# Down projection of a feed-forward block: the readings of sums right behind their product, the tail's low parts behind the last reading

## The chip, the cores and the metric

The kernel runs on one core of one Trainium2 chip. The metric is the time of one execution in microseconds (us) on the device; lower is better. The core has five engines with a queue of instructions each: TensorE (PE, matrix products, with weight loads as PEld), VectorE (DVE), ScalarE (ACT), GpSimd (POOL) and SyncE (SP, here only an issuer of loads).

## The reference

Two layers, each a feed-forward block, a mixer of attention and retention, and a second feed-forward block, every one followed by a layer norm. 512 tokens, width 1024, inner width 2816.

```
def swiglu_ffn(x, w_gu, w_down):
    a, u = jnp.split(x @ w_gu, 2, axis=-1)
    return (jax.nn.silu(a) * u) @ w_down

for l in range(DEPTH):                       # DEPTH = 2
    x = layer_norm(ALPHA * x + 0.5 * swiglu_ffn(x, ffn1_w_gu[l], ffn1_w_down[l]), ln1_g[l], ln1_b[l])
    x = layer_norm(ALPHA * x + hybrid_mixer(x, ...), ln2_g[l], ln2_b[l])
    x = layer_norm(ALPHA * x + 0.5 * swiglu_ffn(x, ffn2_w_gu[l], ffn2_w_down[l]), ln3_g[l], ln3_b[l])
```

There are four feed-forward blocks in all, so four down projections (`@ w_down`), called D1 to D4 here. A mixer follows D1 and D3, the next layer's first feed-forward block follows D2, and nothing follows D4.

## The kernel before

**Split products.** Every float32 product is made of three matmuls: each operand is split into a high part (a cast on ACT, line 161) and a low part (a subtraction on DVE, line 162), and high x high, low x high and high x low are added in PSUM (lines 170 to 172). So each 128 x 1024 unit of weights costs one load into a raw tile (two raw buffers), one cast and one subtraction. The high part is named `uh`, the low part `ul`; `xh` and `xl` are the parts of the other operand.

**The weights' queue.** `Weights` holds the list of all units of the program. `get` hands out the next one, `done` gives buffers back, and both call `pump`, which issues casts and subtractions up to six units ahead (six unit buffers) and loads into raw tiles as they come free. A raw tile comes free when its last subtraction is done.

**The down projection.** The first 16 of 22 chunks of 128 rows are multiplied by a scheme of seven products on quarters of the matrices (numbered n = 0 to 6 in the loop of `ffn`), each of four groups of 12 matmuls with 512 columns. Some products add onto banks of PSUM that hold a sum already; before the bank is used for the next sum, `into` reads it into Y on DVE (line 726). These are the *readings*: two banks each after n = 1, 2, 3 and 5. The last, after n = 5, reads the two banks `low`. Behind product n = 5 PE runs chunk 16 (24 matmuls, the last six of which write `low`), then n = 6, chunk 17, and then the *tail*: chunks 18 to 21, of which each needs a unit of weights in a tail buffer (`tl`) and a split part of the hidden activations hT in a tile `hr`. Layer norm readings (line 459) follow bank by bank.

**The sums of weights.** The tiles R hold quarters of the matrix; POOL issues loads that add another quarter onto them (line 369) once the subtraction that used them is done.

**What sets the order.** Every engine works through its own queue in order. The order in the queues is set by the tile framework's scheduler when the program is built: from the first feed-forward block on (`self.pin = False`) it may move casts, subtractions and readings against each other where no data is in the way. A dependency without synchronisation (`add_manual_dep(..., NOSYNC)`) fixes the order of two instructions of one engine without a wait on a semaphore.

In the lists of instructions below, D1's tiles have these names: `ul_370` and `ul_380` are the low parts of chunks 16 and 17 (both from `raw_308`), `ul_383` and `ul_385` those of chunks 18 and 19 (from `raw_315`), `ul_388` and `ul_391` those of chunks 20 and 21 (from `raw_381`); `ul_372` to `ul_378` are the units of n = 6, `ul_362` to `ul_368` those of n = 5.

Of the kernel before, what the change touches and what calls it, by code (L numbers as in the profile page):

```python
# [10 lines left out]
ALU = mybir.AluOpType  # L11
# [18 lines left out]
GROUPS = 4  # L30
# [8 lines left out]
NOSYNC = mybir.DependencyInfo(mybir.DependencyClass.NoSync, mybir.DependencyReason.DATA)  # L39
# [55 lines left out]
class Trunk:  # L95
# [61 lines left out]
        lo = pool.tile([P, 1024], F32R, tag=tag + "l", name=self.nm("ul"), **kw)  # L157
        return hi, lo

    def split(self, hi, lo, src):  # L160
        a = self.nc.scalar.copy(hi, src)  # L161
        b = self.nc.vector.tensor_sub(lo, src, hi.bitcast(F32))  # L162
        if self.pin:
            self.tc.keep_in_program_order(a)
            self.tc.keep_in_program_order(b)
# [91 lines left out]
    def rows_item(self, w, r0, key, pools, heads=False):  # L257

        def load():
            v = self.raw().rearrange("p (c n) -> p c n", c=2)  # L260
            if heads:
                for kv in range(2):
                    q0 = kv * 256 + r0 // 2
                    self.nc.sync.dma_start(v[kv * HD : (kv + 1) * HD],
                                           w[q0 : q0 + P, :].rearrange("(c p) n -> p c n", p=HD))
            else:
                self.nc.sync.dma_start(v, w[r0 : r0 + 256, :].rearrange("(c p) n -> p c n", p=P))
            return v

        def cut(c):  # L270
            def go(v, hi, lo):
                self.split(hi, lo, v[:, c, :])
                return hi, lo
            return go

        return [(key, load, pools[c], cut(c)) for c in range(2)]
# [205 lines left out]
    def ffn(self, g_, b, out=None):  # L482
        nc, tc, W = self.nc, self.tc, self.W
        with ExitStack() as ctx:
# [4 lines left out]
            hT = hpool.tile([P, NF, SEQ], F32, name=self.nm("hT"))  # L489
# [94 lines left out]
            for fp in range(NFP):  # L584
                if fp == 0:
# [4 lines left out]
                    more = []  # L590
# [46 lines left out]
            def part(m, i, j):  # L637

                f = (j * GROUPS + 2 * m) * 2
                return hT[:, f : f + 4, i * 256 : (i + 1) * 256]  # L640

            def operand(src):

                k = slots[0] = (slots[0] + 2) % KC
                f = src.shape[1]
                hh, hl = (v[:, k : k + 2, :].rearrange("p k t -> p (k t)").rearrange("p (f t) -> p f t", f=f)
                          for v in (self.xh, self.xl))
                self.split(hh, hl, src)
                h = f // 2
                return [(hh[:, q * h : q * h + h], hl[:, q * h : q * h + h]) for q in range(2)]  # L650
# [3 lines left out]
            def fifth(m):  # L654

                a11, a21, a22 = part(m, 0, 0), part(m, 1, 0), part(m, 1, 1)
                nc.vector.tensor_sub(s1, a21, a22)
                nc.vector.tensor_sub(a21, a11, a21)
                nc.vector.tensor_sub(a11, s1, a11)
                return operand(s1)  # L660

            def third(m):

                nc.vector.tensor_add(part(m, 0, 1), part(m, 0, 1), part(m, 0, 0))
                return operand(part(m, 0, 1))

            def operands():
                ms = range(GROUPS // 2)
                for m in ms[1:]:
                    yield from operand(part(m, 0, 1))  # L670
                for m in ms:
                    yield from operand(part(m, 0, 0))
                for m in ms:
                    yield from fifth(m)
                for m in ms:
                    yield from operand(part(m, 0, 0))
                for m in ms:
                    yield from third(m)
                for m in ms:
                    yield from operand(part(m, 1, 0))  # L680
                chunks = operand(hT[:, FIRST : FIRST + 2, :])
                yield chunks[0]
                for m in ms:
                    yield from operand(part(m, 1, 1))
                yield chunks[1]
                for f in range(NF - TAIL, NF, 2):
                    room = pool.tile([P, 2, 2, 512], F32R, tag="hr", name=self.nm("hr"), bufs=2)
                    self.split(room[:, 0], room[:, 1], hT[:, f : f + 2, :])
                    for q in range(2):
                        yield room[:, 0, q : q + 1], room[:, 1, q : q + 1]  # L690

            def seventh(banks, u, h, new):

                for i, b_ in enumerate(banks):
                    ts = slice(i * P, (i + 1) * P)
                    for f in range(2):
                        self.mm3(b_, (h[0][:, f, ts], h[1][:, f, ts]), (u[0][:, f, :], u[1][:, f, :]),
                                 new and f == 0, False, skip_group_check=True)
                self.step()

            def down(f, u, h, t, q):
# [3 lines left out]
                         skip_group_check=True)  # L705

            split = operands()
            ahead = [(hv[0][:, g], hv[1][:, g]) for g in range(2)] + [next(split)]

            def chunk(f):  # L710
                u, h = W.get(), ahead.pop(0)
                ahead.append(next(split))
                for i, (t, q) in enumerate(((0, 0), (0, 1), (1, 0), (1, 1), (2, 1), (3, 1), (2, 0), (3, 0))):
                    down(f, u, h, t, q)
                    if i % 4 == 3:
                        self.step()
                W.done()
# [4 lines left out]
            def into(banks, t0, q, scale, sign=ALU.add):  # L722

                for i, b_ in enumerate(banks):
                    y = self.Y[:, t0 + i, q * 512 : (q + 1) * 512]
                    nc.vector.scalar_tensor_tensor(out=y, in0=y, scalar=scale, in1=b_, op0=ALU.mult, op1=sign)  # L726

            for n, (banks, new, more) in enumerate((
                    (left, True, None), (low, True, (0, 0, ALPHA)), (high, True, (0, 1, ALPHA)),
                    (low, False, (0, 1, 1.0, ALU.subtract)), (right, True, None),  # L730
                    (low, False, (2, 1, ALPHA, ALU.subtract)), (low, False, None))):
                if n == 6:
                    chunk(FIRST)
                for g in range(GROUPS):
                    u, h = W.get(), ahead.pop(0)
                    ahead.append(next(split))
                    seventh(banks, u, h, new and g == 0)
                    W.done(2 if n == 0 and g == 1 else 1)
                if more:
                    into(banks, *more)  # L740
            for f in range(FIRST + 1, NF - TAIL):
                if f == FIRST + 1:
                    gb = self.load_ln(self.spool, g_, b, "S", 2)
# [397 lines left out]
```

## Time and profile before

| | |
|---|---|
| time, median of 3 runs | 1792.26 us (1791.44 to 1794.13) |
| the profiled execution | 1792.29 us, its span 1790.4 us |
| PE busy | 1767.3 us of the span (99%) |
| DVE busy | 1386.6 us (77%) |
| ACT busy | 906.4 us (51%) |
| POOL busy | 162.7 us (9%) |
| granted TensorE clock, mean | 0.998 |
| bytes read from HBM | 206.09 MB |

The span is from the first to the last instruction of the profiled execution; the rest of its time, 1.9 us, lies around it. Rows of a timeline have the start in us from the span's start, the length in us, engine, line, operation, output <- input, shape, count, and in brackets the engine's idle time before and what ended it. `SPq` and `POOLq` mark instructions that issue loads. The last fields of a row of stretches are the granted clock, the share of the DMA engines and GB/s. Spans overlap a little: a matmul is listed as 0.39 us long while the next one starts 0.23 us after it, and a subtraction as 1.22 us with the next one 1.14 us behind.

### The profile page before, as it was taken

How to read it: one execution, taken by the hardware profiler on the slowest of the kernel's cores; microseconds unless marked ns; L12 is line 12 of the kernel's file. 1: busy time of each engine (PE TensorE's matmuls, PEld its weight loads, DVE VectorE, ACT ScalarE, POOL GpSimd, SP SyncE). 2: the span in 40 equal slices, each digit the busy share in tenths (PEclk: the TensorE clock that was granted, in tenths of full speed). 3: DMA queues.
4: the chain of work that ended last, by engine and by line, in shares of the span. 5: the costliest groups of instructions: out<-in, count | busy, mean ns of one | idle time of the engine just before them, and what ended most of it. 6: DMA issues, size and time to landing. Idle time of an engine off the chain costs nothing.

```text
span 1790.4 us, 29087 instructions
## 1 busy us (share of the span) xinstructions
PE 1767.3 (99%) x11978; PEld 1611.0 (90%) x11978; DVE 1386.6 (77%) x1926; ACT 906.4 (51%) x1423; POOL 162.7 (9%) x136
## 2 busy tenths in 40 slices
PE   9999999999999999999999999999999999999998
PEld 9999987887789999998799999889877899999876
DVE  7888888656767888879688887877667687888884
ACT  5455555278722455556235555553785234555550
POOL 0000031111111000012000000301011100000211
PEclk9999999999999999999999999999999999999999
DMA  6234397223222232389313324961323122244961
GB/s 188 95 102 135 120 228 172 88 83 90 52 95 71 86 127 95 95 241 181 118 58 98 106 95 165 224 175 42 99 79 94 48 95 95 95 129 131 217 136 48
DMA packets 158326, 210.07 MB, mean 117 GB/s; under 512 B 4848, under 2 KB 116208, under 8 KB 158192
## 3 DMA queue, kind: packets, MB, share of 16 engines
q1 hardware_dynamic: 140784, 174.64, 30.3%
q0 software_dynamic: 17408, 33.56, 10.5%
q8 instruction: 94, 1.54, 0.4%
q14 instruction: 40, 0.33, 0.1%
HBM read 206.09 MB, written 2.10 MB: 116 GB/s over the span
## 4 chain that ended last, share of the span: by engine, by line
PE 73%; DVE 10%; issue 7%; DMA 4%; ACT 4%; POOL 1%; SPq 0%; POOLq 0%; DVEq 0%; ACTq 0%
PE ps L170 23%; PE ps L171 23%; PE ps L172 23%; DVE ul L162 4%; DMA R<-in_ffn_w_down_dram 2%; DVE xl L162 2%; ACT uh L161 1%; PE ps L435 1%; DMA raw<-in_ffn_w_down_dram 1%; ACT sw L910 1%; DMA raw<-in_ffn_w_gu_dram 1%; ACT b L952 1%; ACT b L946 1%; DVE Y L726 1%; POOL R L369 0%
## 5 line engine op out<-in xcount | busy, mean ns | idle before, releaser
L170 PE MATMUL ps<-xh,uh 128*128 128x256 f32 (+1 forms) x1616 | 482.1, 298 | 0.0
L172 PE MATMUL ps<-xh,ul 128*128 128x256 f32 (+1 forms) x1616 | 479.1, 297 | 0.9 <-DVE ul L162 0.9
L171 PE MATMUL ps<-xl,uh 128*128 128x256 f32 (+1 forms) x1616 | 478.7, 296 | 0.2 <-DVE xl L162 0.2
L161 ACT CAST uh<-raw 128x1024 fp32r<-128x1024 f32 (+1 forms) x285 | 249.2, 894 | 247.9 <-PE ps L171 136.8
L162 DVE TENSOR_TENSOR ul<-raw,uh 128x1024 fp32r<-128x1024 f32 (+1 forms) x285 | 287.6, 1024 | 87.8 <-ACT uh L161 87.5
L170 PE MATMUL ps<-Th,uh 128*128 128x256 f32 x1152 | 319.1, 277 | 0.0
L171 PE MATMUL ps<-Tl,uh 128*128 128x256 f32 x1152 | 318.7, 277 | 0.0
L172 PE MATMUL ps<-Th,ul 128*128 128x256 f32 x1152 | 318.3, 276 | 0.0
L170 PEld LDWEIGHTS ps<-xh,uh 128*128 128x128 f32 x1616 | 307.9, 191 | 10.5 <-issue 1.6
L172 PEld LDWEIGHTS ps<-xh,ul 128*128 128x128 f32 x1616 | 307.8, 191 | 9.8 <-DVE ul L162 1.3
L171 PEld LDWEIGHTS ps<-xl,uh 128*128 128x128 f32 x1616 | 308.0, 191 | 8.4 <-DVE xl L162 0.8
L170 PE MATMUL ps<-uh,xh 128*128 128x512 f32 x672 | 265.1, 394 | 8.2 <-DVE Y L726 8.2
L171 PE MATMUL ps<-ul,xh 128*128 128x512 f32 x672 | 262.2, 390 | 0.0
L172 PE MATMUL ps<-uh,xl 128*128 128x512 f32 x672 | 261.9, 390 | 0.0
L161 ACT CAST uh<-S 128x1024 fp32r<-128x1024 f32 x144 | 151.2, 1050 | 149.0 <-PE ps L171 145.1
L162 DVE TENSOR_TENSOR ul<-S,uh 128x1024 fp32r<-128x1024 f32 x144 | 175.9, 1221 | 60.1 <-ACT uh L161 59.5
L171 PEld LDWEIGHTS ps<-Tl,uh 128*128 128x128 f32 x1152 | 216.7, 188 | 0.0
L170 PEld LDWEIGHTS ps<-Th,uh 128*128 128x128 f32 x1152 | 216.7, 188 | 0.0
L172 PEld LDWEIGHTS ps<-Th,ul 128*128 128x128 f32 x1152 | 216.3, 188 | 0.0
L369 POOL DMA_DIRECT2D R<-in_ffn_w_down_dram x64 | 77.7, 1216 | 994.7 <-DVE ul L162 959.0
L170 PEld LDWEIGHTS ps<-uh,xh 128*128 128x128 f32 x672 | 126.5, 188 | 38.2 <-DVE Y L726 9.9
L172 PEld LDWEIGHTS ps<-uh,xl 128*128 128x128 f32 x672 | 126.4, 188 | 26.6
(143 smaller groups left out, 2391.5 us busy)
## 6 DMA issues: line engine op xcount, KB each, us to landing
raw<-in_ffn_w_gu_dram SPq DMA_DIRECT2D x86, 1024.0 KB, 5.4
R<-in_ffn_w_down_dram POOLq DMA_DIRECT2D x64, 512.0 KB, 7.4
raw<-in_ffn_w_down_dram SPq DMA_DIRECT2D x20, 1024.0 KB, 5.1
raw<-in_w_in_dram SPq DMA_DIRECT2D x18, 1024.0 KB, 5.2
R<-in_ffn_w_down_dram SPq DMA_DIRECT2D x16, 1024.0 KB, 6.4
raw<-in_w_in_dram SPq DMA_DIRECT2D x8, 512.0 KB, 4.6
raw<-in_w_out_dram SPq DMA_DIRECT2D x8, 512.0 KB, 6.2
raw<-in_w_out_dram SPq DMA_DIRECT2D x4, 1024.0 KB, 4.9
```

The source lines that it names most:

```text
L161: a = self.nc.scalar.copy(hi, src)
L162: b = self.nc.vector.tensor_sub(lo, src, hi.bitcast(F32))
L170: mm(out, ah, bh, start=start, stop=False, **kw)
L171: mm(out, ah, bl, start=False, stop=False, **kw)
L172: mm(out, al, bh, start=False, stop=stop, **kw)
L369: self.nc.gpsimd.dma_start(src, rows(i, j, g * 256, 256), accum_op=ALU.add))
L435: nc.tensor.transpose(b[:, c * P : (c + 1) * P], src[:, c * P : (c + 1) * P], self.ident)
L726: nc.vector.scalar_tensor_tensor(out=y, in0=y, scalar=scale, in1=b_, op0=ALU.mult, op1=sign)
L910: nc.scalar.copy(sw[q * 32 : q * 32 + 32, :n], src[o * 32 : o * 32 + 32, :n])
L946: nc.scalar.activation(s[kv][:, cc, :nk], s[kv][:, cc, :nk], AF.Exp, bias=m[:, cc : cc + 1], scale=SCALE, accum_out=den[:, cc : cc + 1])
L952: nc.scalar.activation(s[kv][:, cc, :nk], s[kv][:, cc, :nk], AF.Copy, scale=den[:, cc : cc + 1])
```

## The change

Two edits. `into` is called before `W.done` of a product's last group, so before the units that `W.done` pumps are issued. And the subtractions for the low parts of the tail (the units of chunks 18 to 21, and the two `hr` tiles) get a dependency that places them behind the latest reading recorded at the time they are written, with no semaphore.

```
-    def split(self, hi, lo, src):
+    def split(self, hi, lo, src, behind=None):
         a = self.nc.scalar.copy(hi, src)
         b = self.nc.vector.tensor_sub(lo, src, hi.bitcast(F32))
+        if behind is not None:
+            self.tc.add_manual_dep(b.ins, behind.ins.name, NOSYNC, reason="the reading goes first")
...
-                self.split(hi, lo, v[:, c, :])
+                self.split(hi, lo, v[:, c, :], self.reading if pools[c] == self.tail_units else None)
...
-                    self.split(room[:, 0], room[:, 1], hT[:, f : f + 2, :])
+                    self.split(room[:, 0], room[:, 1], hT[:, f : f + 2, :], self.reading)
...
-                    nc.vector.scalar_tensor_tensor(out=y, in0=y, scalar=scale, in1=b_, op0=ALU.mult, op1=sign)
+                    self.reading = nc.vector.scalar_tensor_tensor(out=y, in0=y, scalar=scale, in1=b_, op0=ALU.mult,
+                                                                  op1=sign)
...
                     seventh(banks, u, h, new and g == 0)
+                    if more and g == GROUPS - 1:
+                        into(banks, *more)
                     W.done(2 if n == 0 and g == 1 else 1)
-                if more:
-                    into(banks, *more)
```

The order of PE's and POOL's instructions is the same in both programs. On DVE, ACT and SP it differs in the four down projections alone, and on DVE at the start of the third feed-forward block too.

DVE in D1, up to the last reading (the two SCALAR_TENSOR_TENSOR), before:

```order
L162 TENSOR_TENSOR xl_78<-hT_14_145,xh_77 128x1024
L162 TENSOR_TENSOR hr_389_3302<-hT_14_145,hr_389_3302 128x1024
L162 TENSOR_TENSOR ul_370_3145<-raw_308_2671,uh_369_3144 128x1024
L162 TENSOR_TENSOR hr_396_3343<-hT_14_145,hr_396_3343 128x1024
L162 TENSOR_TENSOR xl_78<-hT_14_145,xh_77 128x1024
L162 TENSOR_TENSOR ul_372_3163<-R_311_2700,uh_371_3162 128x1024
L162 TENSOR_TENSOR ul_374_3179<-R_311_2700,uh_373_3178 128x1024
L162 TENSOR_TENSOR xl_78<-hT_14_145,xh_77 128x1024
L162 TENSOR_TENSOR ul_376_3197<-R_312_2702,uh_375_3196 128x1024
L162 TENSOR_TENSOR ul_378_3215<-R_312_2702,uh_377_3214 128x1024
L726 SCALAR_TENSOR_TENSOR Y_79<-Y_79,ps_324_2782 128x512
L726 SCALAR_TENSOR_TENSOR Y_79<-Y_79,ps_326_2784 128x512
```

The same place on DVE after the change, and what stands behind the reading now:

```order
L162 TENSOR_TENSOR ul_374_3179<-R_311_2700,uh_373_3178 128x1024
L162 TENSOR_TENSOR xl_78<-hT_14_145,xh_77 128x1024
L162 TENSOR_TENSOR ul_376_3197<-R_312_2702,uh_375_3196 128x1024
L162 TENSOR_TENSOR ul_378_3215<-R_312_2702,uh_377_3214 128x1024
L728 SCALAR_TENSOR_TENSOR Y_79<-Y_79,ps_324_2782 128x512
L728 SCALAR_TENSOR_TENSOR Y_79<-Y_79,ps_326_2784 128x512
L162 TENSOR_TENSOR ul_383_3265<-raw_315_2737,uh_382_3264 128x1024
L162 TENSOR_TENSOR ul_380_3233<-raw_308_2671,uh_379_3232 128x1024
L162 TENSOR_TENSOR ul_385_3281<-raw_315_2737,uh_384_3280 128x1024
L162 TENSOR_TENSOR hr_389_3302<-hT_14_145,hr_389_3302 128x1024
L162 TENSOR_TENSOR hr_396_3343<-hT_14_145,hr_396_3343 128x1024
```

Six subtractions moved from ahead of the last reading to behind it: the two hr from among the ten before it, and the four of chunks 18 to 21 from further up (two ahead of the reading after n = 3, two between the two readings). The two readings after n = 1, which had a subtraction between them, now stand side by side. On ACT the two casts of chunks 20 and 21 moved as well, from ahead of the last two casts of n = 5 to behind the cast of chunk 17.

SP at the end of D2, before (`raw_1115` holds chunks 20 and 21; the `gu` loads are the next feed-forward block's):

```order
L267 DMA raw_1115_8667<-in_ffn2_w_down_dram 128x2x1024
L191 DMA raw_1120_8717<-in_ffn1_w_gu_dram 128x8x256
L448 DMA ln_1129_8772<-in_ln3_g_dram 128x1024
L449 DMA ln_1129_8772<-in_ln3_b_dram 128x1024
L191 DMA raw_1126_8754<-in_ffn1_w_gu_dram 128x8x256
L191 DMA raw_1135_8810<-in_ffn1_w_gu_dram 128x8x256
```

And after:

```order
L450 DMA ln_1129_8772<-in_ln3_g_dram 128x1024
L451 DMA ln_1129_8772<-in_ln3_b_dram 128x1024
L269 DMA raw_1115_8669<-in_ffn2_w_down_dram 128x2x1024
L193 DMA raw_1120_8717<-in_ffn1_w_gu_dram 128x8x256
L193 DMA raw_1126_8754<-in_ffn1_w_gu_dram 128x8x256
L193 DMA raw_1135_8810<-in_ffn1_w_gu_dram 128x8x256
```

The two loads of the layer norm's parameters went ahead of the tail's load. `raw_1115` now takes the buffer of chunks 16 and 17 and waits for chunk 17's subtraction, `raw_1120` that of chunks 18 and 19, `raw_1126` waits for chunk 21's subtraction, and `raw_1135` for the last one from `raw_1120`.

DVE at the end of D2, after the change, from the subtractions of chunks 20 and 21 to the layer norm's first two readings (line 461 there):

```order
L162 TENSOR_TENSOR ul_1122_8732<-raw_1115_8669,uh_1121_8731 128x1024
L162 TENSOR_TENSOR ul_1125_8751<-raw_1115_8669,uh_1124_8750 128x1024
L162 TENSOR_TENSOR ul_1128_8769<-raw_1120_8717,uh_1127_8768 128x1024
L162 TENSOR_TENSOR ul_1132_8803<-raw_1126_8754,uh_1131_8802 128x1024
L162 TENSOR_TENSOR ul_1134_8807<-raw_1120_8717,uh_1133_8806 128x1024
L162 TENSOR_TENSOR ul_1137_8813<-raw_1126_8754,uh_1136_8812 128x1024
L461 SCALAR_TENSOR_TENSOR Y_79<-Y_79,ps_1054_8211 128x512
L463 BN_STATS st_1141_8846<-Y_79 128x6
L162 TENSOR_TENSOR ul_1140_8819<-raw_1135_8810,uh_1139_8818 128x1024
L162 TENSOR_TENSOR ul_1168_9014<-raw_1135_8810,uh_1167_9013 128x1024
L461 SCALAR_TENSOR_TENSOR Y_79<-Y_79,ps_1055_8212 128x512
```

Before, both subtractions from `raw_1135` stood ahead of the norm's first reading; now they stand between its first and its second. Further on, the first norm reading of the fourth token block, which stood ahead of the second pair of `xl` that the third feed-forward block starts with, moved behind it.

## The prediction

> **What bounds the kernel now.** I read the page first, then the waits of PE, then PE's timeline where it waits, and from there back through DVE, ACT, POOL and DMA.
>
> ```profile
> span 1790.4 us, 29087 instructions
> PE 1767.3 (99%) x11978; PEld 1611.0 (90%) x11978; DVE 1386.6 (77%) x1926; ACT 906.4 (51%) x1423; POOL 162.7 (9%) x136
> ...
> raw<-in_ffn_w_gu_dram SPq DMA_DIRECT2D x86, 1024.0 KB, 5.4
> ```
>
> PE is the bound: it is idle for 23.1 us in all. The order of PE's own instructions is not touched, so time can come only from its waits. The largest of these (engine, what it waited for, total us, times, longest) is:
>
> ```profile
> engine line waited for: us in total, times, longest us
> PE ps L170 <- DVE Y L726: 8.2, 4, 3.5
> ```
>
> Line 726 is the reading of a sum; four waits, one in each down projection (D1 to D4), all at the last reading, whose two banks chunk 16 writes next. PE's rows (start, length, [idle before]):
>
> ```profile
> 302.62 0.39 PE L172 MATMUL ps<-uh,xl 128*128 128x512 f32 x1
> 305.02 0.50 PE L170 MATMUL ps<-uh,xh 128*128 128x512 f32 x1 [2.01 <-DVE Y L726]
> 305.36 0.39 PE L171 MATMUL ps<-ul,xh 128*128 128x512 f32 x1
> ...
> 852.68 0.39 PE L172 MATMUL ps<-uh,xl 128*128 128x512 f32 x1
> 855.11 0.50 PE L170 MATMUL ps<-uh,xh 128*128 128x512 f32 x1 [2.04 <-DVE Y L726]
> ...
> 1188.55 0.39 PE L172 MATMUL ps<-uh,xl 128*128 128x512 f32 x1
> 1189.63 0.50 PE L170 MATMUL ps<-uh,xh 128*128 128x512 f32 x1 [0.69 <-DVE Y L726]
> ...
> 1737.32 0.39 PE L172 MATMUL ps<-uh,xl 128*128 128x512 f32 x1
> 1741.21 0.80 PE L170 MATMUL ps<-uh,xh 128*128 128x512 f32 x1 [3.50 <-DVE Y L726]
> 1741.80 0.63 PE L171 MATMUL ps<-ul,xh 128*128 128x512 f32 x1
> ...
> 1744.35 0.40 PE L171 MATMUL ps<-ul,xh 128*128 128x512 f32 x1
> ...
> 1741.20:1744.00 2.80, 2.79 (x7) 2.22 (x8) 1.69 (x2) 0.00 (x0) 0.00 (x0) 0.50 0.09 35
> ```
>
> Undisturbed, one matmul of 512 columns follows another in 0.227 us, so D1's next was due at 302.85: 2.17 lost, and 0.11 more on the first matmul (305.02 to 305.36), 2.28. D2 alike: 2.20 + 0.11 = 2.31. D3: 0.85 + 0.11 = 0.96. D4: 3.66, and then seven matmuls take 3.14 instead of 1.59, since the granted clock is 0.50 in that stretch (the last line, sixth figure before the DMA's): 1.55 more, 5.21. **Sum 10.76.**
>
> **Why the reading is late.** DVE, POOL and ACT before the last reading of D1, and one row of each in D4:
>
> ```profile
> 286.45 2.36 DVE L162 TENSOR_TENSOR ul<-raw,uh 128x1024 fp32r<-128x1024 f32 x2 [0.89 <-ACT uh L161]
> 291.79 1.23 DVE L162 TENSOR_TENSOR ul<-R,uh 128x1024 fp32r<-128x1024 f32 x1 [1.84 <-ACT uh L161]
> 294.07 1.22 DVE L162 TENSOR_TENSOR hr<-hT,hr 128x1024 fp32r<-128x1024 f32 x1
> 295.20 1.22 DVE L162 TENSOR_TENSOR ul<-raw,uh 128x1024 fp32r<-128x1024 f32 x1
> 302.02 2.35 DVE L162 TENSOR_TENSOR ul<-R,uh 128x1024 fp32r<-128x1024 f32 x2
> 304.29 1.27 DVE L726 SCALAR_TENSOR_TENSOR Y<-Y,ps 128x512 f32<-128x512 f32 x2
> ...
> 281.37 1.22 POOL L369 DMA_DIRECT2D R<-in_ffn_w_down_dram  x1 [2.20 <-DVE ul L162]
> 290.71 1.05 ACT L161 CAST uh<-R 128x1024 fp32r<-128x1024 f32 x1 [1.45 <-DMA R<-in_ffn_w_down_dram]
> ...
> 1716.37 1.21 POOL L369 DMA_DIRECT2D R<-in_ffn_w_down_dram  x1 [2.19 <-DVE ul L162]
> 1723.10 2.00 ACT L161 CAST uh<-raw 128x1024 fp32r<-128x1024 f32 x2 [5.21 <-DMA raw<-in_ffn_w_down_dram]
> 1740.48 1.27 DVE L726 SCALAR_TENSOR_TENSOR Y<-Y,ps 128x512 f32<-128x512 f32 x2
> ```
>
> From 291.79 on DVE runs without a gap; the reading is a matter of what is queued ahead. PE would allow it at 299.0: the sixth product's last matmul lies 18 matmuls (4.08 us) before the one at 302.62.
>
> **The change, part by part.**
>
> *Two hr subtractions leave the queue ahead of the last reading.* Each takes 1.13 (294.07 to 295.20). If nothing else moved, the reading of D1 would start at 302.02 and its first bank be free at 302.70 (0.68 each), 0.15 before PE's 302.85. D2 (late by 2.20) and D3 (0.85) are covered by the same 2.27. D4 would keep 3.66 - 2.27 = 1.39 and, with a gap as short as those of D1 and D2, no half clock. So this alone is worth 10.76 - 1.39 = 9.4: the low end.
>
> *Four raw subtractions leave too, two of them with their casts.* On ACT the casts of the last tail pair waited for their load (5.21 in D4) with the casts of the sums R behind them; now they stand behind all of these. The last accumulating load (POOL, 281.37) waited for a subtraction behind two of the raw ones and can start up to 2.27 earlier, and no tail load runs beside it. It took 9.3 us to land (281.37 to 290.71). From its landing to the reading lie a cast and its subtraction (2.4), seven more subtractions (8.0) and about 1.1 us in which one of them waits for ACT: 11.5 us. D4's was issued at 1716.37, so the reading could start at 1716.4 - 2.3 + 9.3 + 11.5 = 1734.9, 2 us before it is needed; D1's at 299.9, 2 us as well. I take the whole 10.76, since D4 lost its time to that 5.21, not to the two hr. High end: the same.
>
> *The first readings stand together,* so one subtraction between them comes 0.6 later. Its product starts 5 us afterwards (three products of 48 matmuls, 10.9 us each, before 298.9 is 266.3): 0. The layer norm's two small loads now stand ahead of the tail load on SP; what they wait for, a sum's last split, comes before what the tail load waits for: 0.
>
> *What is late next: the tail's last pair and the next stage's weights.* Six subtractions follow the reading, and the load of the last tail pair now waits for the second of them. In D1: readings over at 300.3, load out at 302.7, landed (5.4 by the page) at 308.1, split by 310.5. PE wants it after chunk 16, four groups and chunk 17 (298.9 + 5.4 + 10.9 + 5.4 = 320.7): 10 us of cover. But the next stage's loads queue on its buffers. Rows of D2's end, in which the next stage is another feed-forward, and of D1's, with the mixer behind:
>
> ```profile
> 856.81 9.08 SPq L191 DMA_DIRECT2D raw<-in_ffn_w_gu_dram  x2
> 862.05 2.00 ACT L161 CAST uh<-raw 128x1024 fp32r<-128x1024 f32 x2 [4.19 <-DMA raw<-in_ffn_w_gu_dram]
> 871.20 1.05 ACT L161 CAST uh<-raw 128x1024 fp32r<-128x1024 f32 x1 [5.17 <-DMA raw<-in_ffn_w_gu_dram]
> 878.59 0.69 DVE L459 SCALAR_TENSOR_TENSOR Y<-Y,ps 128x512 f32<-128x512 f32 x1 [1.30 <-PE ps L172]
> 895.28 1.28 DVE L162 TENSOR_TENSOR xl<-ps,xh 128x512 fp32r<-128x512 f32 x2
> 896.52 0.28 PE L170 MATMUL ps<-xh,uh 128*128 128x256 f32 x1
> 896.64 0.28 PE L171 MATMUL ps<-xl,uh 128*128 128x256 f32 x1
> ...
> 306.73 6.02 SPq L229 DMA_DIRECT2D raw<-in_w_in_dram  x4
> 312.39 1.05 ACT L161 CAST uh<-raw 128x1024 fp32r<-128x1024 f32 x1 [1.92 <-DMA raw<-in_w_in_dram]
> 324.10 1.23 DVE L162 TENSOR_TENSOR ul<-raw,uh 128x1024 fp32r<-128x1024 f32 x1 [4.18 <-ACT uh L161]
> 325.75 0.69 DVE L459 SCALAR_TENSOR_TENSOR Y<-Y,ps 128x512 f32<-128x512 f32 x1 [0.42 <-PE ps L172]
> 328.47 0.69 DVE L459 SCALAR_TENSOR_TENSOR Y<-Y,ps 128x512 f32<-128x512 f32 x1 [1.30 <-PE ps L172]
> ```
>
> D1: the mixer's second load follows the tail pair's split (310.5, or 311.5 with ACT between), lands 5.6 later (306.73 to 312.39) at 317.1; the third follows the first's split (314.2), lands by about 319.5; the last subtraction ahead of the norm ends at 323.1. The norm's first reading may start at 325.75 - 2.28 = 323.5, its second has 1.30 of idle ahead. No lag: 0, with over 1 us to spare. D3 is the same program; D4 has no next stage.
>
> D2: three loads in a chain. Tail pair out at 852.6, landed 858.0, split 861.4; second out 861.5, landed (5.2, 856.81 to 862.05) 866.7, first two splits by 870.3; third out, landed (5.6, the second issue of the first row, 865.5, to 871.20) at 876.0, split 877.0 to 879.3. Those last two subtractions stand ahead of the norm's second reading, which PE would allow at 878.59 - 2.31 = 876.3: a lag of 3.0, or 4.2 if the tail pair lands 1.2 later beside its neighbour. From there DVE is dense to the xl at 895.28, whose second half ends at 896.56 and is wanted 12 matmuls of 0.12 after 896.52: 1.4 of slack, and the new order has one reading less ahead of it, 0.7 more. So PE waits 3.0 - 2.1 = 0.9 to 2.1 at the start of the third feed-forward: I take 1.3, nearer to the loads as measured one at a time. Bounds: 0 and 4.
>
> **Sum.** 1792.29 (the profiled execution: span 1790.4 and 1.9 around it; the runs' median 1792.26 is the same) - 10.76 + 1.3 = **1782.8 us**.
>
> **A rule weighed.** The row says 0.50 of the clock after 3.66 us without work and full clock after 2.2. The Trainium skill, "TensorE: Matmul & The Clock Gate", Part 1, has the clock halve after an idle window of about 3.4 us that runs freely, so that it depends on phase. The row agrees with the length; on the phase one execution shows nothing. By the row the change is worth 10.76; by the rule a run of before can miss the half clock, and the first rival below is what the time would then be.
>
> **The rivals.**
> - *No half clock in the timed runs.* It hangs on something that differs between executions: 1.55 less to win, 1792.26 - 9.2 + 1.3 = 1784.4. For it: the three runs spread over 2.7 us. Against: median and profiled time agree to 0.03.
> - *Nothing is given back.* D2's loads land faster than one after another at 5.4: lag under 2.1. 1792.29 - 10.76 = 1781.5. For it: DMA is nearly free there. Against: the chain of three has no slack in my sum.
> - *More is given back.* Each landing of the chain takes 0.75 longer: lag 5.9, wait 3.7 at D2's end, D1 and D3 still covered. 1785.2; with a half clock behind it, 1787.
> - *No change.* The accumulating loads land 2 us later than before, not earlier, and hold the cast that DVE needs (as 1.45 at 290.71): the readings stay late, 1792. Against: the load that ran beside them is gone.
> - *Slower.* The next stage's weights become the wait everywhere: each load takes the 9.3 us of the accumulating one. D1 and D3 then lag 3.7 (wait 3.2 each), D2's three loads lag 14.6 (wait 12.5, and 1.5 of half clock): 1792.29 - 10.76 + 20.4 = 1801.9. It turns slower once these waits pass 10.8 together, landings of about 7.7. For it: the chain is real. Against: 5.2 and 5.6 were measured in just that place.
>
> **How the numbers follow.** Likeliest 0.46 (1782.8, own range 1781.8 to 1784); no half clock 0.06; nothing given back 0.25; more given back 0.14; no change 0.05; slower 0.04. The range 1781 to 1787 takes the first four and the low end of the gain (9.4). A difference under 0.2% (3.6 us) can't be told from none: faster 0.91, same 0.05, slower 0.04.
>
> **What the profile after would show.** PE's waits on the reading gone, or one of about 1 us in D4; no stretch at half clock in D4; the last readings starting within 1 us of PE's release; the first xl of the third feed-forward ending after PE wants it, by 1 to 2 us, and no such wait before the mixers. I would be wrong if the readings still wait behind casts of R, or if a wait on ul or xl of over 4 us opens at a stage's start.

## The result and the profile after

| | before | after |
|---|---|---|
| median of six runs each, same chip (us) | 1794.38 | 1782.22 |
| lowest and highest (us) | 1791.44, 1799.89 | 1781.79, 1782.69 |
| profiled execution (us) | 1792.29 | 1781.79 |
| its span, PE busy (us) | 1790.4, 1767.3 | 1780.0, 1764.5 |

The ratio is 0.9932, 95% interval 0.992 to 0.9944: 0.7% faster, by 12.2 us between the medians and 10.5 between the profiled executions. The prediction was 1782.8. The runs of the kernel after lie within 0.9 us of each other, those of before within 8.5; that is a second difference, which a second profile of before, below, explains. Two later executions stand far outside, one of before (1926.2 us) and one with 128 unused bytes (7130.8), and no ratio below counts them.

The page and PE's list of waits, after (what PE waited for, total us, times, longest):

```profile
span 1780.0 us, 29097 instructions
PE 1764.5 (99%) x11978; PEld 1609.9 (90%) x11978; DVE 1387.0 (78%) x1926; ACT 906.7 (51%) x1423; POOL 162.8 (9%) x136
...
PE ps L985 <- DVE yal L162: 2.1, 2, 1.1
PE ps L429 <- POOL ident masks.py:199: 1.4, 1, 1.4
...
PE ps L173 <- DVE xl L162: 0.4, 2, 0.3
PE ps L174 <- DVE ul L162: 0.4, 2, 0.2
```

The row of 8.2 us on the readings is gone; the mixer's own wait (2.1) leads the list. PE at the place of the former gap in D1 and D4 (start, length), then its granted clock in D4 (the figure of 1.00 behind the busy time):

```profile
302.37 0.39 PE L174 MATMUL ps<-uh,xl 128*128 128x512 f32 x1
302.60 0.39 PE L172 MATMUL ps<-uh,xh 128*128 128x512 f32 x1
...
1732.16 0.39 PE L174 MATMUL ps<-uh,xl 128*128 128x512 f32 x1
1732.39 0.39 PE L172 MATMUL ps<-uh,xh 128*128 128x512 f32 x1
...
1732.00:1736.00 4.00, 4.00 (x19) 1.00 0.61 191
```

The matmul that had waited follows its forerunner in 0.23, in D2 and D3 too, and nothing runs at half clock. Why, from DVE in D1, and the last reading of D4:

```profile
297.08 1.23 DVE L162 TENSOR_TENSOR ul<-R,uh 128x1024 fp32r<-128x1024 f32 x1 [0.23 <-ACT uh L161]
298.23 1.28 DVE L728 SCALAR_TENSOR_TENSOR Y<-Y,ps 128x512 f32<-128x512 f32 x2
299.42 3.49 DVE L162 TENSOR_TENSOR ul<-raw,uh 128x1024 fp32r<-128x1024 f32 x3
302.83 2.36 DVE L162 TENSOR_TENSOR hr<-hT,hr 128x1024 fp32r<-128x1024 f32 x2
...
1728.88 1.28 DVE L728 SCALAR_TENSOR_TENSOR Y<-Y,ps 128x512 f32<-128x512 f32 x2
...
1714.65 1.05 ACT L161 CAST uh<-R 128x1024 fp32r<-128x1024 f32 x1 [1.50 <-DMA R<-in_ffn_w_down_dram]
1737.33 2.00 ACT L161 CAST uh<-raw 128x1024 fp32r<-128x1024 f32 x2 [7.76 <-DMA raw<-in_ffn_w_down_dram]
```

The reading stands directly behind the last split that its product needs, and the two hr and the raw ones behind it. In D1 it is over for its first bank at 298.9, 3.7 us before PE's 302.60. In D4 ACT still waits 7.76 us for the tail's load, longer than the 5.21 of before, but with nothing queued behind it that the reading needs.

The two traces can be laid matmul against matmul, since PE's order is the same. Before falls behind by 2.28 in D1, 2.30 in D2, 0.97 in D3 and 5.21 in D4, 10.76 in all. It makes up 0.37 at the start of the third feed-forward and 0.36 in the two mixers, and lost 0.26 more in the first 25 us. That gives 10.3; the last matched matmul is 10.4 apart, the profiled times 10.5.

What was given back stands at the end of D2 (SP, ACT, DVE; then PE at the start of the third feed-forward):

```profile
850.53 0.38 SPq L269 DMA_DIRECT2D raw<-in_ffn_w_down_dram  x1
...
855.50 2.00 ACT L161 CAST uh<-raw 128x1024 fp32r<-128x1024 f32 x2 [7.72 <-DMA raw<-in_ffn_w_down_dram]
...
873.10 2.00 ACT L161 CAST uh<-raw 128x1024 fp32r<-128x1024 f32 x2 [5.88 <-DMA raw<-in_ffn_w_gu_dram]
...
874.18 2.36 DVE L162 TENSOR_TENSOR ul<-raw,uh 128x1024 fp32r<-128x1024 f32 x2 [1.56 <-ACT uh L161]
876.46 0.68 DVE L461 SCALAR_TENSOR_TENSOR Y<-Y,ps 128x512 f32<-128x512 f32 x1
...
892.95 0.68 DVE L162 TENSOR_TENSOR xl<-ps,xh 128x512 fp32r<-128x512 f32 x1
...
893.30 0.28 PE L172 MATMUL ps<-xh,uh 128*128 128x256 f32 x1
893.69 0.39 PE L173 MATMUL ps<-xl,uh 128*128 128x256 f32 x1
```

The chain of loads is there: the last cast waits 5.88 for its load, its two subtractions stand ahead of the norm's second reading. With the 4.65 by which the traces are apart there taken off before's 878.59, that reading would have started at 873.9; it starts at 876.46, a lag of 2.5, and PE loses 0.27 at 893.69, where it waits for the last xl, and 0.1 near it.

### The profile page after: what moved, and what is told of

Read it like the earlier page. It is cut to its first block, busy times and chain, and to the rows that moved or that the text cites. A ratio compares the mean times of both kernels' runs of the same rounds, so it can differ in the third digit from the quotient of the medians.

```text
span 1780.0 us, 29097 instructions
## 1 busy us (share of the span) xinstructions
PE 1764.5 (99%) x11978; PEld 1609.9 (90%) x11978; DVE 1387.0 (78%) x1926; ACT 906.7 (51%) x1423; POOL 162.8 (9%) x136
## 4 chain that ended last, share of the span: by engine, by line
PE 36%; DVE 6%; issue 4%; DMA 2%; ACT 2%; POOL 1%; POOLq 0%; DVEq 0%; SPq 0%; ACTq 0%
PE ps L172 12%; PE ps L174 11%; PE ps L173 11%; DVE ul L162 1%; DMA R<-in_ffn_w_down_dram 1%; DMA raw<-in_w_in_dram 1%; DVE Y L473 1%; DVE st L463 1%; ACT sw L913 1%; DVE xl L162 1%; POOL sw L915 0%; DVE Y L470 0%; DVE Y L461 0%; PE ps L437 0%; ACT uh L161 0%
```

## The experiments

The runs of one call are compared with runs of the kernel before made between them; in the first call that kernel's median was 1796.11, in the second 1794.05, in the third 1795.11, in the fourth 1793.03.

**The place of the readings alone.** The call moves into the loop, and the subtractions are left free:

```diff
+                    if more and g == GROUPS - 1:
+                        into(banks, *more)
                     W.done(2 if n == 0 and g == 1 else 1)
-                if more:
-                    into(banks, *more)
```

> The first edit alone (the call of the reading ahead of done), no dependency. Theory: what makes the last reading late are the six subtractions ahead of it in DVE's queue, and these stay; PE waits on the reading as before, about 2.2, 2.2, 0.9 and 3.7 us in D1 to D4, and the time stays at 1791 to 1796. Rival: the earlier call lets the scheduler put the reading first, and a good part of the 10.5 us is won, 1782 to 1787.

Measured: 1793.71, ratio 0.9982 (0.9969 to 0.9995). PE's wait on the readings, and the two sides of the gap in D2:

```profile
PE ps L172 <- DVE Y L728: 8.4, 4, 2.9
...
856.04 0.50 PE L172 MATMUL ps<-uh,xh 128*128 128x512 f32 x1 [2.53 <-DVE Y L728]
856.38 0.39 PE L173 MATMUL ps<-ul,xh 128*128 128x512 f32 x1
...
858.34 0.63 PE L174 MATMUL ps<-uh,xl 128*128 128x512 f32 x1
```

All four waits stay, 8.4 us against 8.2: this part of the change removes none of them. Its median is 2.4 us below that of before, in runs that spread over 7.6, and no row shows a gain that the edit made. In D2 the matmuls fall to half clock, though not at once: only 1.5 us after PE went on.

**The dependency alone.** The converse: the added dependency, with the call where it was.

> The second edit alone (the dependency of the tail's subtractions), the call of the reading as before. Theory: the whole change is in this edit, 1782.2 within 0.5, no wait of PE on the reading. Rival: the two edits share the gain, then this one stays at 1785 or more.

Measured: 1782.13 (1781.30 to 1783.47), ratio 0.9927 (0.9908 to 0.9945), no wait on a reading. This is the whole change. Its profile tells something of D2's end too: PE comes there 0.7 us earlier than in the kernel after, the norm's second reading starts at the same 876.46, and PE, which waits for an xl until 891.89, loses just these 0.7.

**The dependency on the two hr alone**, which is the first term of the prediction:

```diff
-                self.split(hi, lo, v[:, c, :], self.reading if pools[c] == self.tail_units else None)
+                self.split(hi, lo, v[:, c, :])
```

> The dependency on the two hr subtractions alone; the four raw ones stay ahead of the last reading. My low end: the reading comes 2.27 earlier in each down projection, so no wait in D1 to D3 and about 1.4 us in D4 with no half clock; nothing is given back at D2's end, because the next stage's loads stay as early as before; 1783 (1782.4 to 1783.6). Rival: DVE waits in between for ACT and the two hr were hidden in that, so the waits shrink by less than 2.27; 1786 to 1790.

Measured: 1785.16, ratio 0.9949 (0.9932 to 0.9967), the profiled run 1788.60. PE's wait, D2's gap, and what DVE and ACT waited for ahead of that reading:

```profile
PE ps L172 <- DVE Y L728: 4.2, 3, 2.1
...
853.65 0.50 PE L172 MATMUL ps<-uh,xh 128*128 128x512 f32 x1 [2.06 <-DVE Y L728]
...
854.95 0.63 PE L174 MATMUL ps<-uh,xl 128*128 128x512 f32 x1
...
836.79 2.00 ACT L161 CAST uh<-raw 128x1024 fp32r<-128x1024 f32 x2 [4.43 <-DMA raw<-in_ffn_w_down_dram]
837.87 2.36 DVE L162 TENSOR_TENSOR ul<-raw,uh 128x1024 fp32r<-128x1024 f32 x2 [3.12 <-ACT uh L161]
844.95 1.23 DVE L162 TENSOR_TENSOR ul<-raw,uh 128x1024 fp32r<-128x1024 f32 x1 [0.93 <-ACT uh L161]
```

A miss, and the other way round: D1, D2 and D3 still wait (0.7, 2.2 and 1.8), D4 hardly (0.3). The 2.27 of the two hr leave the queue, but in D2 DVE spends as much idle (3.12 and 0.93 above, where before had 1.89 and none), since the raw ones still stand in it and wait for casts, and these for the tail's load. Whether D1 to D4 are covered hangs on when that load lands: from its issue to its cast it took 6.6, 8.9, 9.6 and 6.9 us in D1 to D4 here, and 6.6, 7.6, 6.5 and 9.4 in the first profile of before.

**The dependency on the four raw alone:**

```diff
-                    self.split(room[:, 0], room[:, 1], hT[:, f : f + 2, :], self.reading)
+                    self.split(room[:, 0], room[:, 1], hT[:, f : f + 2, :])
```

> The dependency on the four raw subtractions alone; the two hr stay ahead of the last reading. In the changed kernel the reading starts at 298.2 in D1 and PE needs its first bank at 302.85; two hr more put the start at 300.5, its end at 301.2. Theory: either half of the dependency is enough in D1 to D3, and this half also in D4: no waits, 1782.2 within 0.7, and the small wait at the start of the third feed-forward (0.3) stays. Rival: the hr casts hold ACT and so the reading; waits of about 1 us stay in each, 1785 to 1787.

Measured: 1784.48, ratio 0.994 (0.9918 to 0.9963). PE's list has no reading in it, and the norm's second reading at D2's end stands here:

```profile
PE ps L173 <- DVE xl L162: 1.3, 4, 0.3
...
875.62 2.36 DVE L162 TENSOR_TENSOR ul<-raw,uh 128x1024 fp32r<-128x1024 f32 x2 [2.13 <-ACT uh L161]
877.90 0.68 DVE L461 SCALAR_TENSOR_TENSOR Y<-Y,ps 128x512 f32<-128x512 f32 x1
```

The raw ones alone remove all four waits. The time is 2.3 us more than the whole change, where I had expected the same. Laid against the kernel after, PE loses nothing in D1 to D4, 0.6 in the first 25 us, 0.6 at the start of the third feed-forward, and 1.0 in the mixers. The readings come 1.8 later (300.06 in D1), of which 0.6 is PE's own delay by then, so the tail's load goes out later, and at D2's end the norm's second reading (0.9 off for the distance of the traces up to there) is 0.6 later than in the kernel after; PE pays 0.6 more for it. The two hr serve the stage that comes next, not the readings.

**The kernel before, profiled a second time.**

> The kernel before, profiled once more, unchanged. If the half clock hung on a gap of 3.4 us or more, D1 and D2 (gaps of 2.2) run on at full clock and D4 alone shows a stretch at half clock, as in the first profile: within 1 us of 1792.3. If it hangs on where the gap lies in a period that runs freely, another of the four gaps may show it or D4 may miss it (1.6 us each, up or down); a gap itself may differ where a load lands at another time.

Measured: 1796.76. PE at the readings of D1 and D2, the clock in all four places, and D1's clock in the first profile of before:

```profile
305.25 0.63 PE L170 MATMUL ps<-uh,xh 128*128 128x512 f32 x1 [2.08 <-DVE Y L726]
305.68 0.63 PE L171 MATMUL ps<-ul,xh 128*128 128x512 f32 x1
...
858.57 0.80 PE L170 MATMUL ps<-uh,xh 128*128 128x512 f32 x1 [3.38 <-DVE Y L726]
...
305.20:309.00 3.80, 3.75 (x10) 0.55 0.22 69
858.50:862.00 3.50, 3.43 (x8) 0.52 0.23 64
1195.10:1198.00 2.90, 2.82 (x12) 1.00 0.34 126
1745.50:1749.50 4.00, 3.90 (x10) 0.57 0.09 35
```

```profile
305.00:308.80 3.80, 3.78 (x17) 1.00 0.21 63
```

The same gap in D1, 2.2 us (305.25 here, 305.02 there), is followed by 10 matmuls in 3.8 us at a clock of 0.55 in this execution, by 17 at full clock in that one. D2's gap has grown from 2.2 to 3.5, D4's has shrunk from 3.7 to 2.3, and both have half clock behind them. The tail's load took 9.1 instead of 7.6 us in D2 and 8.2 instead of 9.4 in D4, about the differences of these two gaps; in D1, 1.3 more of landing changed the gap by 0.1 only.

What decides about the clock is in the traces. Within an execution the starts of all stretches at half clock, the one behind the last matmul too, lie whole multiples of 3.413 us apart: in this one they are at 305.46, 858.42, 1745.88 and 1790.26, so 162, 260 and 13 multiples. Each stretch behind a gap lasts 3.413 us, or about 1.7 of work lost. So the clock is set anew on a raster of slots of 3.413 us, and a gap can be laid against it (a gap counts from where the next matmul was due, and idle is the part of it that falls into one slot):

| execution, place | gap | most idle in one slot | the next slot |
|---|---|---|---|
| before, D4 | 3.66 | 3.36 | half clock |
| before again, D2 | 3.54 | 3.38 | half clock |
| readings alone, D4 | 3.09 | 2.38 | half clock |
| before again, D4 | 2.33 | 2.33 | half clock |
| before again, D1 | 2.25 | 2.25 | half clock |
| hr alone, D2 | 2.23 | 2.19 | half clock |
| readings alone, D2 | 2.69 | 1.88 | half clock |
| before, D2 | 2.20 | 1.67 | full clock |
| before again, D3 | 1.44 | 1.44 | full clock |
| hr alone, D3 | 1.78 | 1.33 | full clock |
| before, D1 | 2.17 | 1.13 | full clock |

A gap of 2.2 us that fills most of a slot halves the clock, and one that the raster cuts in two does not; the line lies between 1.67 and 1.88 us idle, near half a slot. The clock goes down at the end of the slot, which is why the matmuls behind a gap may first run at full speed.

Three stretches instead of one, and gaps of which two hang on a landing: so the runs of before lie anywhere from 1788 to 1801 over all the calls. The mean clocks fit, of which a stretch costs 0.001: 0.999 in five runs of 1787.9 to 1790.0, 0.996 in twenty of 1795.0 to 1798.0, and 0.995 in the two slowest, 1799.1 and 1800.6. The kernel after has neither such gaps nor stretches.

**Statistics ahead of the last reading**, six, eight and ten of them, which were meant to make gaps of set length, and **four behind it**, to make the tail late:

```diff
+                if t0 == 2:
+                    w = self.small.tile([P, 6], F32, tag="w8", name=self.nm("w8"), bufs=1)
+                    for _ in range(8):
+                        d = nc.vector.bn_stats(out=w, in_=banks[0])
...
+                        tc.add_manual_dep(d.ins, self.held.ins.name, NOSYNC, reason="one behind the other")
```

> The changed kernel with six statistics of 512 columns on DVE (some 0.7 us each, their result unused) between the last split that the reading needs and the last reading of each down projection. The reading of D1 was over for its first bank at 298.9 and wanted at 302.6, so six hold PE for about 1.2 us in each of D1 to D4. Everything behind the readings is late by 4.2, PE by 1.2, so 3.0 more of lag in the next stages: 3.0 more at D2's end, 0.5 at D1's and D3's. Both theories: 1782.2 + 4.8 + 4.0 = 1791, no stretch at half clock, and times that lie as close together as those of the changed kernel (within 1 us).

> As with six, but eight: gaps of about 2.6 us in PE in each of D1 to D4; without half clock 1782.2 + 10.4 + 4.0 = 1796.6. Theory A (the clock halves only after a gap of about 3.4 us, all of it idle): no half clock in any execution, times within 1 us of each other. Theory B (it hangs on where the gap lies in a period that runs freely, and gaps of 2.2 to 2.7 can do it): one to three of the four gaps have about eight matmuls at half clock behind them, 1.6 us each, other ones from execution to execution: median about 1800, runs spread over 3 us and more, as those of the kernel before do.

> As with six, but ten: gaps of about 4.1 us in each of D1 to D4; without half clock 1782.2 + 16.4 + 4.0 = 1802.6. Both theories have half clock behind all four gaps, 6.4 us: 1809, and times close together again (within 2 us), since nothing is left to chance. If the spread stays wide, something other than the half clock makes it.

> The changed kernel with four statistics of 512 columns on DVE (2.8 us) behind the last reading of each down projection and ahead of the tail's low parts: the reading is not held, the tail is. By the prediction's chain the lag at D2's end grows from 2.5 to 5.3 against 2.2 of slack: PE waits 3.1 there instead of 0.3. D1 and D3 had 0.4 to spare at the norm's second reading and 2.1 of slack behind it: 0.3 each. 1782.2 + 2.8 + 0.6 = 1785.6. The rival, that D2's 0.3 is not the chain's lag but belongs to the start of the stage, gives 1782.2 to 1783.

Measured: 1802.22, 1800.07, 1800.90 and 1798.97, ratios 1.0043, 1.0031, 1.0035 and 1.0028 (intervals of 0.0012 to 0.0014 to each side at most). None of them tells what it was made for, for two reasons. With eight, DVE reads the sum in D1 here, and PE's list of waits has no reading in it:

```profile
305.22 3.62 DVE L730 BATCH_NORM_STATS2 w<-ps 128x6 f32<-128x512 f32 x5
308.76 1.27 DVE L736 SCALAR_TENSOR_TENSOR Y<-Y,ps 128x512 f32<-128x512 f32 x2
```

This kernel's PE runs 3.8 us behind the kernel after by then, so the reading is 6.7 later, 3.0 past what PE allowed. But the scheduler, which knows of the statistics, has put 15 matmuls of chunk 17 (3.4 us) ahead of chunk 16's six that need the reading's banks, and PE loses nothing in D1 and D3, 0.4 in D2 and 0.3 in D4. No gap worth the name, so no clock to be seen, and a side result: PE had other work with which to cover a late reading.

The second reason is where the time went. All four lose some 4.1 us in each stretch of matmuls of 256 columns (the gate and up projections, 16.3 of the 16.4 by which the profile with eight is longer), not at a wait but evenly. PE in 120 us of the second feed-forward's, of the kernel after and of the one with four statistics behind the reading (x is the number of matmuls):

```profile
640.00:760.00 120.00, 120.00 (x1035) 1.00 0.35 108
```

```profile
646.00:766.00 120.00, 120.00 (x1011) 1.00 0.33 106
...
882.11 2.36 DVE L163 TENSOR_TENSOR ul<-raw,uh 128x1024 fp32r<-128x1024 f32 x2 [0.92 <-ACT uh L162]
884.39 0.68 DVE L464 SCALAR_TENSOR_TENSOR Y<-Y,ps 128x512 f32<-128x512 f32 x1
```

2.3% fewer at the same clock, with about the same DMA share. By operands, the matmuls of Th and Tl take 0.118 from one to the next instead of 0.114, those of xh and xl 0.120 as before. By the addresses in the built programs, the statistics' small tile had pushed all tiles allocated later up by 32 bytes, Th and Tl among them, while uh, ul, xh and xl had stayed.

The run with four behind the reading still tells something of D2, though the opposite of what was meant: the scheduler let one low part go ahead of three of the four, the tail's load went out 0.8 earlier, the norm's second reading (884.39, less the 8.55 that PE is behind there) stands at 875.84, 0.6 earlier than in the kernel after, and the wait at 893.69 is gone. With the runs of the four raw and of the dependency alone that makes three points beside the kernel after, the reading taken against PE each time: 0.6 earlier, PE wins 0.4, all that there was; 0.6 later, it pays 0.6 more; 0.7 later, 0.7 more. So the time given back there is the chain's lag, as the prediction had it.

**Unused bytes behind Y**, to test that the place of the tiles made the 16 us:

```diff
         self.Y = self.base.tile([P, NT, D], F32, name="Y")
+        self.gap = self.base.tile([P, 16], F32, name="gap")
```

> The changed kernel with 64 unused bytes per partition behind Y, so that all tiles allocated later (raw, uh, ul, and the tiles of the stages, hT, Th and Tl among them) lie 64 higher; xh, xl and Y stay. The order of all instructions stays. In the four runs with statistics the added small tile had moved hT, Th and Tl by 32 and not uh and xh: the matmuls of 256 columns of Th and Tl then took 0.118 from one to the next instead of 0.114, those of xh and xl 0.120 as before, and with 3450 of the former that is the 16 us which those runs lost. Theory A (the distance between the moving tile and the weights counts, modulo 512: Th lies 64 below uh, xh at 0): xh now lies 64 below uh as well, some 4200 of its matmuls in the feed-forwards gain 0.0055 each, 23 us, others in the mixers up to 1700 x 0.006 = 10: 1750 to 1760. Theory B (the address of the moving tile alone, modulo 128: Th at 96 is fast, xh at 32 and Th at 0 are not): Th comes to 32, xh stays at 32, and Th loses 3450 x 0.0055 = 19: 1801.

> As before, with 128 unused bytes. Theory A: xh lies 128 below uh; Th and uh keep their distance of 64 and their 0.114. If the gain grows with the distance (0.1195 at 0, 0.1183 at 32, 0.114 at 64), xh falls to 0.114 or under: 1750 to 1760 or less; if 64 is the best distance, something between 1755 and 1782. Theory B: all addresses stay the same modulo 128: 1782.

> The changed kernel with 96 unused bytes per partition behind Y: xh and xl lie 96 below uh and ul, Th and Tl still 64 below. Measured so far from one matmul of 256 columns of xh to the next: 0.1195 at a distance of 0, 0.1142 at 64, 0.1188 at 128 (Th at 32: 0.1183). If 64 is the best and the cost rises evenly on both sides, 0.1165 here: some 4200 x 0.003 = 12.6 won against the changed kernel in the feed-forwards; the matmuls of 512 columns lose, from 0.2268 at 0, 0.002 at 64 and 0.0055 at 128, so some 0.0035 x 2000 = 7: 1776, between 1763.4 and 1782.2. If the best lies between 64 and 128, under 1763. If only multiples of 64 count, as at 0: 1782 to 1792.

Measured: with 64 bytes 1763.44 (1763.32 to 1763.53), ratio to before 0.9821 (0.9804 to 0.9837); with 128, 1791.90, 0.9984 (0.9974 to 0.9995); with 96, 1788.78, 0.9977 (0.9966 to 0.9989). PE in the same stage and in 20 us of D1's products, with 64 bytes and with 128:

```profile
634.00:754.00 120.00, 120.00 (x1062) 1.00 0.37 119
258.00:278.00 20.00, 20.00 (x89) 1.00 1.11 197
```

```profile
640.00:760.00 120.00, 120.00 (x1035) 1.00 0.33 106
262.00:282.00 20.00, 20.00 (x88) 1.00 1.10 195
```

From one matmul to the next in us, the mean over each trace, by the distance in bytes at which the moving tile lies below its weights (modulo 512, from the addresses in the built programs):

| distance | 256 columns | from |
|---|---|---|
| 0 | 0.1195 | xh, xl in the kernel after |
| 32 | 0.118 | Th, Tl with the statistics |
| 64 | 0.114; 0.114 | Th, Tl in the kernel after; xh, xl with 64 bytes |
| 96 | 0.118 | xh, xl with 96 bytes |
| 128 | 0.119 | xh, xl with 128 bytes |

Th and Tl stay at 64 and, on average, at 0.113 to 0.115 in all three, though their own addresses move. So the moving tile's address alone (theory B) is out, and so is that of the weights: in the kernel after, xh and Th meet the same uh at 0.1195 and 0.114. The distance orders what was measured, with 64 the one good value of the five; 0 and 128 are nearly alike, and so are 32 and 96. The time with 64 lies 3 above what I had expected, those with 96 and 128 by 13 and 10: I had expected 96 to lie halfway, and had not counted that the down projections' matmuls of 512 columns, whose distance turns with it, get slower, from 0.227 at 0 to 0.229 at 64 and 0.232 to 0.233 at 96 and 128. With 64 bytes the four gate and up stages win some 5.2 us each and the rest loses about 2.5. This version beats both kernels, without a change in the order of any instruction: 31.7 us less than before's median in the same call, and 18.8 less than the kernel after's, which was not run beside it.

## Why the prediction was right

- *PE's waits and their size.* The 10.76 worked out from before's rows is what the two traces show place by place. That the half clock of D4 (1.55) would go with the gap held as well.
- *The raw subtractions carry it, not the hr.* The step from D4's 5.21 on ACT to "all four readings are early" held: the dependency on the raw ones alone clears all four places. The readings stand at 298.23 in D1 and 1728.88 in D4, where I had 299.9 and 1734.9, which is 1729.7 when the 5.2 by which before is behind there are taken off. That D4 came out so near is luck in part: its last load of sums landed in 6.1 us and not in 9.3, and from there to the reading it took 14.2 and not 11.5.
- *The step that failed: two hr alone win 9.4.* I took DVE's row without a gap in D1 for a queue in which 1.13 less is 1.13 earlier. Without the hr, DVE waited for casts instead, and D1 to D3 kept 0.7, 2.2 and 1.8 while D4 kept 0.3. The low end of the gain was wrong in each of the four places, and that the time came out 9.2 us under before all the same, by its ratio, is luck; the forecast did not rest on it.
- *The first readings together, the norm's loads ahead:* 0 for the first, as the place of the readings alone shows (no loss in its rows). The second comes with the dependency and was not tried apart; PE's list of waits after the change has no parameter of the norm in it.
- *D2 gives back 1.3.* The mechanism was right (the chain's lag less what the norm leaves over), the term was too large: lag 2.5 instead of 3.0 to 4.2, price 0.37. The slack of 2.1 held; the three loads of the chain landed in 5.0 to 5.2 us each, where I had taken 5.2 to 5.6, and of my range of 0.9 to 2.1 I had not taken the low end either. This 0.9 is most of the difference between 1782.8 and 1781.8; the 0.36 that the mixers gave back and the 0.26 of the first 25 us, neither of them in the sum, nearly cancel, which is luck.
- *D1 and D3 give back nothing.* The norm's second reading in D1 waited for PE, as I had it; the mixers gave back 0.36 together, further in.
- *PE would allow the reading at 299.0.* It was too late by more than 1 us: the product's last six matmuls write the second bank only, and the first reading ran at 298.23 without harm.
- *The rule weighed.* The Trainium skill, "TensorE: Matmul & The Clock Gate", Part 1, has a window of about 3.4 us that runs freely, and the clock halve after an idle one. On the phase it was right, with a raster of 3.413 us in these traces, and my row was one draw: the same 2.2 us in D1 left the clock at 1.00 in one execution and at 0.55 in the next. A window that is idle throughout is not needed, though: 1.88 us of one were enough, and 1.67 were not. So the rival that hung on it had the wrong sign. I had let a run of before miss D4's half clock; in the second profile D1 and D2 have it too, the median of before is 1793 and more in every later call, and the gain between medians is 12.2 instead of 10.5.

## What to carry to other kernels

An engine's list of waits names the instruction that came late; what to move is found by asking which instructions stand ahead of it in its queue and themselves wait for something slow, here casts behind a load, and not which are most. A gap on PE that fills more than half of a slot of 3.4 us costs some 1.7 us beyond its length, and which gaps do differs from one execution to the next; a kernel without them shows it in the spread of its runs. Before an experiment that adds a tile is read, see that its matmuls run at the same pace as before, since a shift of 32 bytes cost more here than the whole change won.

## What the runs showed of the hardware

- The clock halves on a raster. Starts of stretches at half clock lay whole multiples of 3.413 us apart within each of four executions (up to 435 multiples), and each stretch at a gap lasted 3.413 us. A slot in which PE was idle for 1.88 us or more was followed by half clock (seven cases), one with 1.67 or less was not, so the same gap of 2.2 us did it or did not by where it fell.
- The distance of 64 bytes between the moving tile and the weights is worth 5% of a matmul of 256 columns (0.114 against 0.1195). With 512 columns, distance 0 was the best of those tried (0.227 against 0.229 to 0.233). What in the memory makes it was not tried, nor, with 256 columns, distances above 128.
- DMA landings of 1 MB: 5.0 to 5.2 us one after another at D2's end, 8.9 for the tail's load in D2 with the hr alone (out at 827.9, cast at 836.8), which was 7.6 in the kernel before. The last load of sums in D4, of 512 KB, took 6.1 (9.3 in D1 before).
